# Fourteen instead of thirteen of the sixteen pairs of the second mixer matrix by products over halves, and an earlier fetch of the gate tiles' weights

## The chip, the cores and the metric

The kernel runs on one core of a Trainium2 chip. The metric is the device time of one execution in microseconds (us); less is better. Before the change, three runs gave 1724.98 us in the median (1724.34 to 1728.57).

## The reference

One step of a decoder layer for 1024 prompt tokens and 8 x 4 sample tokens, that is 1056 tokens together, with a model width of 1024. Everything is float32.

```
h  = RMSNorm(x);  p = h @ w_in        # columns: q | k | v | conv input | z | a | b | gate_A | gate_B
branch A: stick-breaking attention, 8 heads x 64, strictly causal
branch B: short conv + SiLU, gated delta rule, 4 heads with a 128x128 state
m = sigmoid(gate_A) * (o_A @ w_pa) + sigmoid(gate_B) * (o_B @ w_pb);   x = x + m @ w_o
x = x + relu(RMSNorm(x) @ w_up)^2 @ w_down                             # 1024 -> 4096 -> 1024
y = RMSNorm(x)
```

gate_A and gate_B are 1024 columns each. The two matrices of the channel mixer, w_up (1024 x 4096) and w_down (4096 x 1024), are what most of the change is about.

## The kernel before, in words

**A dense product.** Each float32 operand is split into a rounded part and the rest (ScalarE copies to the rounded type, VectorE subtracts), and a product is three TensorE matmuls for each block of 128 of the contraction: high x high, high x low, low x high. This is `dense`, L134 to L139, so nearly all matmuls of the program have one of the lines L137, L138, L139, and the tile names tell the stages apart: `pd_g` gate tiles, `sc`/`wt`/`po` attention, `pb`/`pa` the merge, `px` out projection, `pu` w_up, `pw` w_down by products, `pv` w_down directly. Results go to PSUM banks, and ScalarE or VectorE empties these.

**Gate tiles.** The sixteen 128-column tiles of gate_A and gate_B go through `proj_steps` (L232): the first step of a tile calls `load_w` (L118), which takes a staging tile (tag `wst`, one buffer), issues the DMA on SyncE's queue (L123) and then splits into `wh` and `wl` (L127 on ScalarE, L128 on VectorE, two buffers each, so the split of a tile needs the matmuls of the tile two before it to be done). Then come 4 token blocks of 24 matmuls each; each result goes through a sigmoid on ScalarE (L1042), and the tile is stored (L1044). The first eleven tiles stand ahead of the attention's main loop; the other five are "fills", cut into steps and spread over 34 attention blocks (`pipeline`, L1028). `stage_a` computes the scores four blocks ahead of their use; with a head's first block it loads that head's q, k and v (`attn_load` L914 with the DMAs of L923 to L925, `load_v` L964, its DMA L966), and ScalarE empties the scores through a sigmoid (L939). `residual_step` brings x in (L1049) and writes it out transposed. The order of the instructions on each engine comes from the program's order, from priorities (`tc.high_priority()`) and from a list scheduler that runs a timeline model; each engine and SyncE's DMA queue then take their instructions strictly in that order.

**w_up.** The 32 column tiles of 128 hidden units form 16 pairs (f, f+16), and the tokens come in two groups g. For the pairs from 3 on in both groups, and for the first three with g = 1, both halves of the contraction, of the hidden units and of the tokens are combined into 7 products over halves in the place of 8 (Strassen in Winograd's form, `up_products` L1373). The first NPL = 3 pairs are done directly for g = 0 (`up_plain`, L1332), because the pools of the products aren't there yet. What follows is relu and square (L1394, L1395). For the pairs from NPL on, four VectorE subtractions (L1399 to L1402) make the seven combinations of the hidden values that the w_down products need, stored to DRAM as `hc_d` (L1403). The first three pairs are stored as plain hidden values, `h_d`.

**w_down.** The 13 pairs from 3 on are done in groups of 4, 4 and 5 pairs (L1527): for each of the 7 products i, the group's combinations are loaded (`load_h`, L1455 with the DMA of L1457, split at L1452/L1453), the weights are loaded by quarter (L1465), combined (L1472 to L1476) and split (`weight_part` L1470, L1479/L1480), and 8 PSUM tiles accumulate over the pairs of the group; VectorE adds them to `acc` or `ys`. The buffers: 12 tiles for the combinations, 8 for the split weights, 5 for each quarter. In the first group, a load waits its turn behind the earlier one (`queued`), and the loads of product 0 are issued by GpSimd. The other six tiles (pairs 0 to 2) follow directly: weights loaded and split at L1586 to L1588, hidden values `hp`, then four token stages of 8 column blocks with 18 matmuls each (`pv`), each stage followed by the final norm, the transposes (`fin`) and the store.

Of the kernel before, what the change touches and what calls it, by code (L numbers as in the profile page):

```python
# [8 lines left out]
F32 = mybir.dt.float32  # L9
# [9 lines left out]
P = 128  # L19
D = 1024  # L20
# [18 lines left out]
def hybrid_step(ctx, tc, x_prompt, x_sample, cache_k, cache_v, page_table, state_conv, state_ssm,  # L39
# [78 lines left out]
    def load_w(src, name, wp=wpool, st=None):  # L118
        nk = 8 if st is not None else src.shape[1]
        if st is None:  # L120
            st = wp.tile([P, 8, P], F32, tag="wst", name=f"ws_{name}", bufs=1)
            stv = st if nk == 8 else st.rearrange("p a b -> p (a b)").rearrange("p (k c) -> p k c", k=nk)
            wq[0] = SY.dma_start(stv, src)  # L123
        hi = wp.tile([P, 8, P], F32R, tag="wh", name=f"wh_{name}")
        lo = wp.tile([P, 8, P], F32R, tag="wl", name=f"wl_{name}")
        with tc.high_priority():
            S_.activation(hi, st, AF.Copy)  # L127
            V.tensor_tensor(lo, st, hi.bitcast(F32), op=ALU.subtract)  # L128
        if nk != 8:
            hi = hi.rearrange("p a b -> p (a b)").rearrange("p (k c) -> p k c", k=nk)  # L130
            lo = lo.rearrange("p a b -> p (a b)").rearrange("p (k c) -> p k c", k=nk)
        return hi, lo
# [96 lines left out]
                      [xhc[c][:, k] for k in range(KT)], [xlc[c][:, k] for k in range(KT)], n)  # L229
                evac(c, o, n, pt)  # L230

    def proj_steps(col, name, evac, done):  # L232
        ws = []

        def step(c, o, n):
            if not ws:
                ws.append(load_w(winv[:, :, col:col + P], name))
            wh, wl = ws[0]
            pt = dtile(f"pd_{name}_{c}", True)
            dense(pt, [wh[:, k] for k in range(KT)], [wl[:, k] for k in range(KT)],  # L240
                  [xhc[c][:, k] for k in range(KT)], [xlc[c][:, k] for k in range(KT)], n)
# [795 lines left out]
    def gate_steps(j, b):  # L1037
        gt = fk.tile([P, T], F32, tag="ft", name=f"gt{b}_{j}", bufs=NFT)

        def ev(c, o, n, pt):  # L1040
            with tc.high_priority():
                S_.activation(gt[:, o:o + n], pt[:, :n], AF.Sigmoid)  # L1042

        return proj_steps(3592 + b * D + j * P, f"g{b}_{j}", ev, lambda: SY.dma_start((gA_d, gB_d)[b][j], gt))  # L1044

    def residual_step(t):
        n = P if t < 8 else NS
# [172 lines left out]
    wuv = w_up[0].rearrange("(k p) n -> p k n", p=P)  # L1220
    wdv = w_down[0].rearrange("(k p) n -> p k n", p=P)
    h_d = dr.tile([FF // P, P, T], F32, name="h_d")
    NPL = 3
    hc_d = dr.tile([FF // P // 2 - NPL, 7, P, HN], F32, name="hc_d")

    def by_group(ap, g):
        return ap.rearrange("p (h g n) -> p g h n", h=2, g=2)[:, g]
# [100 lines left out]
    def next_bank(name):  # L1328
        bank[0] += 1
        return mk4[bank[0] % 4](name)  # L1330

    def up_plain(f, g):  # L1332
        wh, wl = load_8(wuv[:, :, f * P:(f + 1) * P], f"up{f}")
        t = up_.tile([P, 7, QN], F32, tag="t", name=f"tp{f}{g}")[:, 0:2]
        for h, (i, ii) in enumerate(((0, 1), (7, 6))):
            pt = next_bank(f"pu{f}{g}_{h}")
            dense(pt, wh, wl, [Xh[g][i][:, k] for k in range(4)] + [Xh[g][ii][:, k] for k in range(4)],
                  [Xl[g][i][:, k] for k in range(4)] + [Xl[g][ii][:, k] for k in range(4)], QN)
            S_.activation(t[:, h], pt[:, :QN], AF.Relu)
        S_.activation(t, t, AF.Square)  # L1340
        SY.dma_start(by_group(h_d[f], g), t)

    def up_weights(f):
        a = wop.tile([P, 8, P], F32, tag="wh", name=f"ua{f}")
# [28 lines left out]
    def up_products(w7, f, g):  # L1373
        pts = []
        for i in range(7):
            pt = next_bank(f"pu{f}{g}_{i}")
            dense(pt, w7[i][0], w7[i][1], [Xh[g][i][:, k] for k in range(4)], [Xl[g][i][:, k] for k in range(4)], QN)
            pts.append(pt[:, :QN])
        p1, p2, p6, p7, p5, p4, p3 = pts

        t = up_.tile([P, 7, QN], F32, tag="t", name=f"t{f}{g}")
        u1, u2 = t[:, 2], t[:, 5]
        S_.activation(u1, p1, AF.Copy)
        with tc.high_priority():
# [5 lines left out]
            V.tensor_tensor(t[:, 1], u2, p4, op=ALU.subtract)  # L1390
            V.tensor_tensor(t[:, 3], p3, u1, op=ALU.add)
        rows = (t[:, 0:4:3], t[:, 1:7:5])
        for r in range(2):
            S_.activation(rows[r], rows[r], AF.Relu)  # L1394
            S_.activation(rows[r], rows[r], AF.Square)  # L1395
            if f < NPL:
                SY.dma_start(by_group(h_d[f + NF * r], g), rows[r])
        if f >= NPL:
            V.tensor_tensor(t[:, 4], t[:, 3], t[:, 0], op=ALU.subtract)  # L1399
            V.tensor_tensor(t[:, 3], t[:, 6], t[:, 3], op=ALU.subtract)  # L1400
            V.tensor_tensor(t[:, 2], t[:, 6], t[:, 4], op=ALU.subtract)
            V.tensor_tensor(t[:, 5], t[:, 2], t[:, 1], op=ALU.subtract)  # L1402
            SY.dma_start(hc_d[f - NPL, :, :, g * QN:(g + 1) * QN].rearrange("i p n -> p i n"), t)  # L1403

    out_proj(0)
    blocks(0)
# [10 lines left out]


    norm(1)
    for f in range(NPL):  # L1420
        up_plain(f, 0)
        up_plain(f + NF, 0)
    kxctx.close()
    u7a = pool("u7a", stack=uctx)
    for f in range(NPL, NF):
        w7 = up_weights(f)
        for g in range(2):
            up_products(w7, f, g)
        if f < 2 * NPL:
            up_products(up_weights(f - NPL), f - NPL, 1)  # L1430
    uctx.close()
    xg_ctx[1].close()
    woctx.close()
# [90 lines left out]
            last_q[0] = r if hasattr(r, "ins") else hq[0]  # L1524
        return r

    groups = [list(range(3, 7)), list(range(7, 11)), list(range(11, 16))]  # L1527
    for gi, fs in enumerate(groups):
        qs2 = [quarters(f) for f in fs]
        if gi:  # L1530
            for q, f in zip(qs2, fs):
                for nm in PARTS:
                    queued(lambda: load_part(q, f, nm), False)
        for i in range(7):

# [12 lines left out]
            if gi == 0 and i == 0:  # L1548
                ys[:] = [fp.tile([P, T], F32, name=f"y{j}") for j in range(KT)]
            if gi == 0 and i in YLOAD:  # L1550
                j0, h = YLOAD[i]
                for j in range(j0, j0 + HJ):
                    queued(lambda: SY.dma_start(half(ys[j], h), half(x1_d[j], h)))
            for j in range(HJ):
                if gi == 0 and i in (0, 2, 3, 4):
                    acc[i, j] = acp.tile([P, HN], F32, name=f"acc{i}_{j}")
                cs_ = slice(j * P, (j + 1) * P)
                for n in range(2):
                    ns_ = slice(n * QN, (n + 1) * QN)
                    pt = next_bank(f"pw{gi}{i}_{j}{n}")  # L1560
                    dense(pt, [w[:, 0, cs_] for w in ws], [w[:, 1, cs_] for w in ws], [h[:, 0, ns_] for h in hs],
                          [h[:, 1, ns_] for h in hs], QN)
                    dst = targets(i, j)[:, ns_]
                    with tc.high_priority():
                        if gi == 0 and i in (0, 2, 3, 4):
                            S_.activation(dst, pt[:, :QN], AF.Copy)
                        elif i == 5:
                            V.tensor_tensor(dst, dst, pt[:, :QN], op=ALU.subtract)
                        else:
                            V.tensor_tensor(dst, pt[:, :QN], dst, op=ALU.add)  # L1570
                if gi == len(groups) - 1:
                    combine(i, j)
# [94 lines left out]
```

## Time and profile before

| | us |
|---|---|
| median of three runs | 1724.98 |
| the profiled execution, its own time | 1733.34 |
| its span, first to last instruction | 1731.6 |
| TensorE busy in the span | 1682.5 |
| VectorE busy | 1153.2 |
| ScalarE busy | 773.3 |
| GpSimd busy | 200.4 |

The profiled execution is one run under the profiler. Times in its rows count from the start of its span. "PE" is TensorE's matmuls, "PEld" its weight loads, DVE VectorE, ACT ScalarE, POOL GpSimd, SPq SyncE's DMA queue. A matmul's recorded duration (283 ns at 264 columns) is longer than the distance to the next one, since matmuls are pipelined; the distance is read from a window (time over count). A row of a wait names the waiting engine, its tile and line, what it waited for, the sum, the number of waits and the longest. In rows of a timeline, the bracket at the end is the engine's idle time ahead of that instruction and what ended it.

### The profile page before, as it was taken

How to read it: one execution, taken by the hardware profiler on the slowest of the kernel's cores; microseconds unless marked ns; L12 is line 12 of the kernel's file. 1: busy time of each engine (PE TensorE's matmuls, PEld its weight loads, DVE VectorE, ACT ScalarE, POOL GpSimd, SP SyncE). 2: the span in 40 equal slices, each digit the busy share in tenths (PEclk: the TensorE clock that was granted, in tenths of full speed). 3: DMA queues.
4: the chain of work that ended last, by engine and by line, in shares of the span. 5: the costliest groups of instructions: out<-in, count | busy, mean ns of one | idle time of the engine just before them, and what ended most of it. 6: DMA issues, size and time to landing. Idle time of an engine off the chain costs nothing.

```text
span 1731.6 us, 34630 instructions
## 1 busy us (share of the span) xinstructions
PE 1682.5 (97%) x13958; PEld 1624.7 (94%) x13958; DVE 1153.2 (67%) x2309; ACT 773.3 (45%) x1542; POOL 200.4 (12%) x243
## 2 busy tenths in 40 slices
PE   7999999999998999999999999999999999999998
PEld 6999999999998788988989989999999999999998
DVE  6665677867243317778766487887777679788743
ACT  5553434343324214564443456554454564344353
POOL 1120111110005114444400000000000000000000
PEclk9999999999999999999999999999999999999999
DMA  5142233234346478977134645555443766433411
GB/s 179 44 122 69 67 107 92 93 118 133 119 138 211 131 185 200 209 196 193 32 118 125 179 140 145 149 148 160 152 137 113 259 217 218 148 117 95 136 68 66
DMA packets 259036, 239.24 MB, mean 138 GB/s; under 512 B 55890, under 2 KB 217011, under 8 KB 258876
## 3 DMA queue, kind: packets, MB, share of 16 engines
q1 hardware_dynamic: 253926, 226.27, 43.9%
q0 software_dynamic: 3200, 10.52, 1.9%
q8 instruction: 110, 1.80, 0.4%
q10 hardware_dynamic: 1750, 0.23, 0.1%
q14 instruction: 50, 0.41, 0.1%
HBM read 163.21 MB, written 73.77 MB: 137 GB/s over the span
## 4 chain that ended last, share of the span: by engine, by line
PE 88%; DMA 4%; DVE 4%; issue 2%; ACT 1%; SPq 0%; DVEq 0%; POOLq 0%; ACTq 0%
PE pu L139 6%; PE pu L137 6%; PE pu L138 6%; PE pw L139 5%; PE pw L138 5%; PE pw L137 5%; PE pd_g L137 3%; PE pd_g L139 3%; PE pd_g L138 3%; PE wt L111 2%; PE po L985 2%; PE pv L137 1%; PE pv L139 1%; PE pv L138 1%; PE px L138 1%
## 5 line engine op out<-in xcount | busy, mean ns | idle before, releaser
L139 PE MATMUL pu<-Xh,ul 128*128 128x264 f32 x812 | 230.1, 284 | 0.0
L137 PE MATMUL pu<-Xh,uh 128*128 128x264 f32 x812 | 229.8, 283 | 0.0
L138 PE MATMUL pu<-Xl,uh 128*128 128x264 f32 x812 | 229.7, 283 | 0.0
L137 PE MATMUL pw<-hc,w 128*128 128x264 f32 x728 | 204.1, 284 | 2.4 <-ACT w L1479 2.4
L138 PE MATMUL pw<-hc,w 128*128 128x264 f32 x728 | 204.6, 285 | 0.0
L139 PE MATMUL pw<-hc,w 128*128 128x264 f32 x728 | 200.8, 285 | 1.0 <-DVE w L1480 1.0
L137 PEld LDWEIGHTS pu<-Xh,uh 128*128 128x128 f32 x812 | 153.2, 189 | 0.1
L138 PEld LDWEIGHTS pu<-Xl,uh 128*128 128x128 f32 x812 | 152.6, 188 | 0.0
L137 PE MATMUL pd_g<-xh,wh_g 128*128 128x256 f32 (+1 forms) x512 | 150.6, 294 | 1.5 <-issue 1.5
L139 PEld LDWEIGHTS pu<-Xh,ul 128*128 128x128 f32 x812 | 152.0, 188 | 0.0
L138 PE MATMUL pd_g<-xl,wh_g 128*128 128x256 f32 (+1 forms) x512 | 149.4, 292 | 1.8 <-issue 1.8
L139 PE MATMUL pd_g<-xh,wl_g 128*128 128x256 f32 (+1 forms) x512 | 149.6, 292 | 1.1 <-issue 1.1
L137 PEld LDWEIGHTS pw<-hc,w 128*128 128x128 f32 x728 | 136.8, 188 | 2.6 <-ACT w L1479 2.6
L138 PEld LDWEIGHTS pw<-hc,w 128*128 128x128 f32 x728 | 136.2, 188 | 0.0
L139 PEld LDWEIGHTS pw<-hc,w 128*128 128x128 f32 x728 | 134.3, 188 | 1.4 <-DVE w L1480 1.4
L947 DVE TENSOR_TENSOR_SCAN pr<-am 128x127 f32<-128x127 f32 (+7 forms) x64 | 87.9, 1376 | 42.7 <-POOL am L943 42.6
L139 PEld LDWEIGHTS pd_g<-xh,wl_g 128*128 128x128 f32 x512 | 98.0, 191 | 5.9 <-issue 5.7
L137 PEld LDWEIGHTS pd_g<-xh,wh_g 128*128 128x128 f32 x512 | 97.9, 191 | 4.7 <-issue 4.0
L138 PEld LDWEIGHTS pd_g<-xl,wh_g 128*128 128x128 f32 x512 | 97.9, 191 | 2.6 <-issue 2.0
L1479 ACT ACTIVATE w<-a 128x512 fp32r<-128x512 f32 x78 | 43.4, 620 | 88.4 <-PE pw L139 77.0
L139 PE MATMUL px<-mh,wl_wo 128*128 128x264 f32 x256 | 72.4, 285 | 1.3 <-DVE wl_wo L1231 1.2
L138 PE MATMUL px<-ml,wh_wo 128*128 128x264 f32 x256 | 72.6, 285 | 0.0
(577 smaller groups left out, 5071.1 us busy)
## 6 DMA issues: line engine op xcount, KB each, us to landing
hc_d<-t SPq DMA_DIRECT2D x26, 924.0 KB
hc<-hc_d SPq DMA_DIRECT2D x87, 264.0 KB
a<-in_w_down_dram SPq DMA_DIRECT2D x48, 256.0 KB
ws_g<-in_w_in_dram SPq DMA_DIRECT2D x16, 512.0 KB
ws_wo<-in_w_o_dram SPq DMA_DIRECT2D x32, 256.0 KB
ua<-in_w_up_dram SPq DMA_DIRECT2D x16, 512.0 KB
ub<-in_w_up_dram SPq DMA_DIRECT2D x16, 512.0 KB
gA_d<-gt SPq DMA_DIRECT2D x8, 528.0 KB
```

Source lines behind the costliest of these rows:

```text
L111: PE.transpose(out, in_, ident[:k, :k])
L137: PE.matmul(pt[:, :n], lhsT=wh[k], rhs=xh[k], start=(k == 0), stop=False)
L138: PE.matmul(pt[:, :n], lhsT=wh[k], rhs=xl[k], start=False, stop=False)
L139: PE.matmul(pt[:, :n], lhsT=wl[k], rhs=xh[k], start=False, stop=(k == nk - 1))
L947: V.tensor_tensor_scan(pr[:, n - 1:0:-1], am_r, am_r, 1.0, op0=ALU.mult, op1=ALU.bypass)
L985: PE.matmul(po[64 * r:64 * r + 64, 0:P], lhsT=vn[:, b, rs], rhs=wts[hh, 2 * m + r][:, b * P:(b + 1) * P], start=(b == 0), stop=(b == 2 * m ...
L1479: S_.activation(tl[:, 0], src, AF.Copy)
```

## The change

Two edits in one. First, NPL is split: NPU = 3 says how many pairs of w_up are done directly for g = 0, as before; NPL = 2 says from which pair on w_down goes by products, so pair 2 moves from the direct part to the products (14 pairs in groups of 4, 5 and 5). `up_plain` therefore does both tiles of a pair in one call and, for pair 2, makes the combinations. The weights' splits of the first product of the first group get high priority. Second, the gate tiles' weights: after the split of one tile, the DMA of the next one is issued at once (in the program's order), not at the first step of the next tile.

```diff
-    def proj_steps(col, name, evac, done):
+    ahead_w = {}
+
+    def fetch_w(col):
+        ahead_w[col] = wpool.tile([P, 8, P], F32, tag="wst", name=f"ws_c{col}", bufs=1)
+        SY.dma_start(ahead_w[col], winv[:, :, col:col + P])
+
+    def proj_steps(col, name, evac, done, next_col=None):
         ws = []

         def step(c, o, n):
             if not ws:
-                ws.append(load_w(winv[:, :, col:col + P], name))
+                if col not in ahead_w:
+                    fetch_w(col)
+                ws.append(load_w(None, name, st=ahead_w[col]))
+                if next_col is not None:
+                    fetch_w(next_col)
...
-    NPL = 3
+
+    NPU, NPL = 3, 2
...
+    def combos(f, g, t):
+        V.tensor_tensor(t[:, 4], t[:, 3], t[:, 0], op=ALU.subtract)
+        V.tensor_tensor(t[:, 3], t[:, 6], t[:, 3], op=ALU.subtract)
+        V.tensor_tensor(t[:, 2], t[:, 6], t[:, 4], op=ALU.subtract)
+        V.tensor_tensor(t[:, 5], t[:, 2], t[:, 1], op=ALU.subtract)
+        SY.dma_start(hc_d[f - NPL, :, :, g * QN:(g + 1) * QN].rearrange("i p n -> p i n"), t)
+
     def up_plain(f, g):
...
+        t = up_.tile([P, 7, QN], F32, tag="t", name=f"tp{f}{g}")
+        rows = (t[:, 0:4:3], t[:, 1:7:5])
+        for r in range(2):
+            wh, wl = load_8(wuv[:, :, (f + NF * r) * P:(f + NF * r + 1) * P], f"up{f}{r}")
...
+            S_.activation(rows[r], rows[r], AF.Square)
+            if f < NPL:
+                SY.dma_start(by_group(h_d[f + NF * r], g), rows[r])
+        if f >= NPL:
+            combos(f, g, t)
...
-    for f in range(NPL):
+    for f in range(NPU):
         up_plain(f, 0)
-        up_plain(f + NF, 0)
...
-    groups = [list(range(3, 7)), list(range(7, 11)), list(range(11, 16))]
+    groups = [list(range(2, 6)), list(range(6, 11)), list(range(11, 16))]
...
-            ws = [weight_part(q, f, i) for q, f in zip(qs2, fs)]
+            with tc.high_priority() if gi == i == 0 else ExitStack():
+                ws = [weight_part(q, f, i) for q, f in zip(qs2, fs)]
```

More of the change, by code (lines that the diff above doesn't have):

```diff
@@ L1042, in ev, with col @@
                 S_.activation(gt[:, o:o + n], pt[:, :n], AF.Sigmoid)
-        return proj_steps(3592 + b * D + j * P, f"g{b}_{j}", ev, lambda: SY.dma_start((gA_d, gB_d)[b][j], gt))
+        def col(j, b):
+            return 3592 + b * D + j * P
+        return proj_steps(col(j, b), f"g{b}_{j}", ev, lambda: SY.dma_start((gA_d, gB_d)[b][j], gt),
+                          None if (j, b) == (KT - 1, 1) else col(*((j, 1) if b == 0 else (j + 1, 0))))
     def residual_step(t):
@@ L1330, in next_bank @@
         return mk4[bank[0] % 4](name)
-    def up_plain(f, g):
[L1333 to L1341, printed above, removed]
+    def combos(f, g, t):
[4 more added lines that the diff above has]
+        SY.dma_start(hc_d[f - NPL, :, :, g * QN:(g + 1) * QN].rearrange("i p n -> p i n"), t)
+    def up_plain(f, g):
+        t = up_.tile([P, 7, QN], F32, tag="t", name=f"tp{f}{g}")
+        rows = (t[:, 0:4:3], t[:, 1:7:5])
+        for r in range(2):
+            wh, wl = load_8(wuv[:, :, (f + NF * r) * P:(f + NF * r + 1) * P], f"up{f}{r}")
+            for h, (i, ii) in enumerate(((0, 1), (7, 6))):
+                pt = next_bank(f"pu{f}{g}{r}_{h}")
+                dense(pt, wh, wl, [Xh[g][i][:, k] for k in range(4)] + [Xh[g][ii][:, k] for k in range(4)],
+                      [Xl[g][i][:, k] for k in range(4)] + [Xl[g][ii][:, k] for k in range(4)], QN)
+                S_.activation(rows[r][:, h], pt[:, :QN], AF.Relu)
+            S_.activation(rows[r], rows[r], AF.Square)
[3 more added lines that the diff above has]
+            combos(f, g, t)
     def up_weights(f):
@@ L1398, in up_products @@
         if f >= NPL:
[L1399 to L1403, printed above, removed]
+            combos(f, g, t)
     out_proj(0)
@@ L1419, in hybrid_step @@
     norm(1)
-    for f in range(NPL):
+    for f in range(NPU):
         up_plain(f, 0)
-        up_plain(f + NF, 0)
     kxctx.close()
     u7a = pool("u7a", stack=uctx)
-    for f in range(NPL, NF):
+    for f in range(NPU, NF):
         w7 = up_weights(f)
@@ L1428, in hybrid_step @@
             up_products(w7, f, g)
-        if f < 2 * NPL:
-            up_products(up_weights(f - NPL), f - NPL, 1)
+        if f < 2 * NPU:
+            up_products(up_weights(f - NPU), f - NPU, 1)
     uctx.close()
```

## The prediction

> **What bounds the kernel now.** I read the page's busy table and its chain first, then windows of the product stages, then TensorE's waits.
>
> ```profile
> PE 1682.5 (97%) x13958; PEld 1624.7 (94%) x13958; DVE 1153.2 (67%) x2309; ACT 773.3 (45%) x1542; POOL 200.4 (12%) x243
> PE 88%; DMA 4%; DVE 4%; issue 2%; ACT 1%; SPq 0%; DVEq 0%; POOLq 0%; ACTq 0%
> ...
> 1410.00:1500.00 90.00, 90.00 (x739) 90.00 (x738) 66.32 (x127) 39.42 (x74) 0.00 (x0) 1.00 0.53 179
> 1500.00:1640.00 140.00, 140.00 (x1149) 140.00 (x1148) 119.02 (x228) 57.15 (x96) 0.00 (x0) 1.00 0.37 118
> ...
> PE sc L937 <- ACT s L939: 4.2, 1, 4.2
> PE pw L137 <- ACT w L1479: 2.4, 1, 2.4
> PE pw L139 <- DVE w L1480: 1.0, 2, 0.5
> PE pv L137 <- ACT wd L1587: 0.9, 2, 0.7
> PE pv L139 <- DVE wd L1588: 0.3, 1, 0.3
> ```
>
> TensorE bounds it: 97% busy, 88% of the chain. So an edit pays in two ways only: fewer matmuls, or a TensorE wait that goes. In the two windows of w_down's products TensorE is never idle, and a matmul of 264 columns comes every 90.00/739 = 0.1218 us (140.00/1149 gives the same). Five rows of waits lie where the change touches the program: 4.2 us in the attention's start, 2.4 and 1.0 in the first group of w_down, 0.9 and 0.3 at the start of its direct part.
>
> A wait can cost more than its length:
>
> ```profile
> 652.60:656.00 3.40, 3.03 (x13) 2.84 (x13) 2.17 (x3) 2.13 (x5) 2.76 (x4) 0.50 0.80 122
> ...
> 1652.60:1656.00 3.40, 3.40 (x17) 3.40 (x17) 1.77 (x6) 1.88 (x4) 0.00 (x0) 0.52 0.00 0
> ```
>
> The seventh number is the granted clock. Right after the 4.2 us wait, and right after those of the direct part, stand 3.4 us at half clock: in the second, 17 matmuls instead of some 28. At half clock, the busy 3.03 us of the first cost about 1.5 us, and the 3.40 of the second (clock 0.52) 1.6.
>
> **Part 1: the matmuls of pair 2.**
>
> ```profile
> L137 PE MATMUL pw<-hc,w 128*128 128x264 f32 x728 | 204.1, 284 | 2.4 <-ACT w L1479 2.4
> L137 PE MATMUL pv<-hp,wd 128*128 128x264 f32 x192 | 55.9, 291 | 0.9 <-ACT wd L1587 0.9
> 1359.77 0.43 DVE L1399 TENSOR_TENSOR t<-t 128x264 f32<-128x264 f32 x1 [1.39 <-ACT t L1395]
> hc_d<-t SPq DMA_DIRECT2D x26, 924.0 KB
> 1075.00:1370.00 295.00, 293.13 (x2412) 292.93 (x2412) 220.17 (x480) 146.47 (x258) 4.38 (x8) 1.00 0.49 151
> 1670.54 0.52 ACT L1614 ACTIVATE y<-y,vec 128x264 f32<-128x264 f32 x1
> ```
>
> Three lines of 728 matmuls for 13 pairs are 2184, or 168 a pair; three of 192 for six direct tiles are 576, or 96 a tile. Pair 2 adds 168 and takes away 2 x 96 = 192: 24 fewer, 24 x 0.1218 = **2.9 us**. All of them are on the path.
>
> What comes with it lies beside other work. Eight more subtractions (four for each token group) are 8 x 0.43 = 3.4 us of VectorE in the w_up stage, where it is busy 220 of 295 us; uncovered they'd cost those 3.4. The store of a token group has seven pieces, 924 KB, where the plain hidden values have four of these, 528 KB: 0.8 MB more in all, and the loads grow by the same, under DMA shares of 0.49 and 0.53. At the 151 GB/s of that window it is 5 us each if uncovered. Splits move from the direct part into product stages where ScalarE has half its time free. Groups of 5 are no new load: the window from 1500 to 1640 lies in such a group, and TensorE is full there. New is that two of them follow each other with five buffers for each quarter of the weights, so that none is spare at the change of groups: the last quarter of the second group is split by the start of its seventh product, and the third group needs it for its second product, two products or 2 x 120 x 0.1218 = 29 us later, while five loads of 256 KB at the 179 GB/s of the 1410 window take 7.3; that is the price if the cover fails. In the direct part, a column block shrinks from 18 to 12 matmuls, 1.46 us; ScalarE has two operations for it, of which the longer takes 0.52, so at most 1.04: TensorE still sets the pace. I take nothing for all of these.
>
> **Part 2: the fetch of the gate tiles.** ScalarE and SyncE's queue at the start of the attention:
>
> ```profile
> 616.40 0.37 SPq L123 DMA_DIRECT2D ws_g<-in_w_in_dram  x1
> 626.67 0.38 SPq L966 DMA_DIRECT2D vn<-v_d  x1
> 632.30 0.78 SPq L1049 DMA_DIRECT2D xr<-in_x_prompt_dram  x1
> 633.12 0.47 SPq L923 DMA_DIRECT2D qs<-qh_d  x1
> 637.98 0.45 SPq L925 DMA_DIRECT2D kl<-kl_d  x1
> 639.17 0.39 SPq L123 DMA_DIRECT2D ws_g<-in_w_in_dram  x1
> ...
> 631.08 1.23 DVE L128 TENSOR_TENSOR wl_g<-ws_g,wh_g 128x1024 fp32r<-128x1024 f32 x1 [4.96 <-ACT wh_g L127]
> 642.24 0.73 ACT L939 ACTIVATE s<-sc,sbb 128x128 f32<-128x128 f32 x2
> 651.39 1.06 ACT L127 ACTIVATE wh_g<-ws_g 128x1024 fp32r<-128x1024 f32 x1 [8.42 <-DMA ws_g<-in_w_in_dram]
> ...
> 639.17 12.14 DMA ws_g<-in_w_in_dram
> ...
> 625.00:655.00 30.00, 25.82 (x200) 25.33 (x199) 6.17 (x9) 7.34 (x15) 3.08 (x8) 0.96 0.94 227
> ```
>
> The chain of the 4.2 us: the thirteenth tile's weights are issued at 639.17, behind six loads of the second head (633.12 to 637.98), and land 12.14 us later, since the DMA engines are 0.94 busy at 227 GB/s. ScalarE's split of them is queued ahead of the emptying of the scores (L939) and stands for 8.42 us; TensorE runs out of free banks and waits. The staging buffer had been free since 631.08 + 1.23 = 632.31. With the fetch written right after the split of the tile before, its place is there, ahead of the second head. Six loads of 256 KB, 1.57 MB, at 227 GB/s are 6.9 us: it lands at about 651.3 - 6.9 = 644.4. ScalarE then stands from 642.24 + 0.73 = 642.97 to 644.4, some 1.5 us instead of 8.4, and since 8.4 cost TensorE 4.2, there are 4.2 us of slack: the wait goes, 4.2 + 1.5 = **5.7 us**. The bounds are 0 (the fetch stays where it is) and 5.7.
>
> What it is moved past: the second head's six loads land up to 2.3 us later (0.52 MB at 227 GB/s). Its scores come after the first head's, whose buffers are free for the third head at 668.33, so some 15 us remain:
>
> ```profile
> 668.33 0.45 SPq L924 DMA_DIRECT2D kh<-kh_d  x1
> ...
> 655.00:765.00 110.00, 110.00 (x894) 98.86 (x894) 81.26 (x77) 57.27 (x126) 45.17 (x63) 1.00 0.82 185
> ```
>
> Next late after that is TensorE's own work: from 655 to 765 it is never idle. The last three tiles' loads come sooner too; what they pass on the queue is x and its transposed stores, which only the out projection reads. For the tiles before the thirteenth the edit changes little, since the DMA of the next one already comes right after a split (the one at 616.40, say).
>
> **Part 3: priority for the first splits of w_down.**
>
> ```profile
> 1367.18 0.65 ACT L1394 ACTIVATE t<-t 128x528 f32<-128x528 f32 x1 [3.78 <-DVE t L1390]
> 1369.86 1.13 ACT L1479 ACTIVATE w<-a 128x512 fp32r<-128x512 f32 x2
> 1375.57 5.64 SPq L1465 DMA_DIRECT2D a<-in_w_down_dram  x8
> 1382.23 0.69 DVE L1472 TENSOR_TENSOR s<-a,a 128x512 f32<-128x512 f32 x1 [3.23 <-DMA a<-in_w_down_dram]
> 1405.52 3.10 DVE L1480 TENSOR_TENSOR w<-a,w 128x512 fp32r<-128x512 f32 x5
> 1380.00:1400.00 20.00, 20.00 (x166) 20.00 (x165) 16.24 (x30) 9.37 (x20) 0.00 (x0) 1.00 0.96 349
> ```
>
> Before, ScalarE idles 3.78 us, then empties w_up's last pair, and only at 1369.86 splits the weights that TensorE waits for. With priority the splits fit into that idle time, and the 2.4 us go from there. But the third product, 30 us later, hangs on quarters issued from 1375.57 on; at 1382.23 VectorE waits for these, the DMA engines are 0.96 busy, and VectorE works through to 1405.52, where TensorE waits 1.0 us now. None of this comes sooner, so TensorE, 2.4 us earlier, will wait 2.4 us longer there. I take **0**, between a gain of 3.4 (both waits go) and a loss of 2.3 (four splits of 1.13/2 in front of the emptying of the last pair, which delays its store and the queue behind it).
>
> **Part 4: the start of the direct part.**
>
> ```profile
> 1625.30 14.85 SPq L1586 DMA_DIRECT2D wds<-in_w_down_dram  x9
> 1645.45 0.33 SPq L1586 DMA_DIRECT2D wds<-in_w_down_dram  x1
> ```
>
> Twelve weight loads become eight. They start once w_down's last products let the queue go (1625.30) and went at 14.85/9 = 1.65 us each, so the eighth is issued near 1638.5 instead of 1645.45 for the twelfth, 7 us sooner. The second half's first use comes sooner by 4 blocks of 6 matmuls, 2.9 us. That leaves 4 us against waits of 0.9 + 0.3 = 1.2: they go, and with them the half clock, 1.2 + 1.6 = **2.8 us**; bounds 0 and 2.8.
>
> The Trainium skill, page "TensorE: Matmul & The Clock Gate", section "HAM oscillation — how this bites in real kernels", says that the clock falls to half after an idle gap of more than about 3.4 us. The 4.2 us wait agrees; the 1.2 us in pieces that stand before the window at 1652.6 don't, so the page would look for another cause of that one.
>
> **Sum.** 2.9 + 5.7 + 0 + 2.8 = 11.4 us. The profiled execution took 1733.34 us, its span 1731.6; the median is 1724.98, so 8.4 us of the profiled one aren't in an ordinary run, and a wait or two may be larger in the profile than without it. I subtract from the median and leave that to the range: 1725.0 - 11.4 = **1713.6 us**, and 1710.2 to 1715.9 with the bounds of part 3.
>
> **The rivals.** About 0.3%, 5.2 us, can be told from no change.
>
> - The fetch doesn't get ahead: the scheduler keeps it behind the second head, because in its model the split ends later than it does on the chip. For it: split and first load are 0.8 us apart. Then 2.9 + 2.8 = 5.7: 1719.3. Chance 0.15.
> - The wait of the direct part stays, because hidden values and weights share ScalarE: 2.9 + 5.7, 1716.4. Chance 0.10.
> - The half clock at 1652.6 isn't due to that wait and stays: 1.6 less, 1715.2. Against it: it follows the waits directly. Chance 0.06. This is what the Trainium skill's page, in the section named above, would make of it.
> - Both waits stay: 2.9 alone, 1722.1. Chance 0.11.
> - Slower: the fetch is queued too far ahead. SyncE takes its queue in order; a fetch put ahead of the first head's loads (626.67) stands there until the staging buffer is free at 632.31, and the first head's q, k, v and the x tile behind it come 5.6 us later. TensorE then waits for the first scores, 5.6 + 1.5 for the clock: -2.9 - 2.8 + 7.1, 1726.4. It decides from about 4.2 us of standing. Standing at L123 is seen at both ends:
>
> ```profile
> SPq L123 <- DVE us L346: 68.8, 6, 24.9
> SPq L123 <- DVE wl_g L128: 6.2, 5, 3.2
> ```
>
> Waits for this very split were at most 3.2 us; the longest of any weight fetch was 24.9, which would give 1725.0 - 5.7 + 24.9 + 1.5 = 1745.7. Chance 0.13.
>
> **How the numbers follow.** The forecast keeps 0.45. Faster by over 5.2 us: 0.45 + 0.10 + 0.06, and of the first rival (5.7 us) 0.09: 0.70. Within: the rest of that, 0.06, the 0.11 and about half of the last, 0.06: 0.23. Slower: 0.07. The range, 1709.5 to 1725.5, holds the forecast with its bounds and four rivals, and leaves out most of the fifth.
>
> **What would show it.** 2352 `pw` and 384 `pv` matmuls at 0.122 us; the thirteenth `ws_g` issued near 632 to 633 and no `sc` wait of 4 us; clock 1.0 from 650 to 660; no `pw` wait at the first product, but 2 to 3 us at the third; no `pv` waits for `wd`. I am wrong if a new TensorE wait of over 3 us stands anywhere, or if the thirteenth fetch still follows the second head's loads.

## The result, and the profile after

In runs beside the kernel before, the changed kernel took 1715.79 us (median of 5; the kernel before 1726.84): the ratio of times is 0.9929, 95% interval 0.9916 to 0.9943. By the medians 11.05 us are gone, by the ratio 12.3 (9.8 to 14.5); the forecast was 11.4. A later set of the changed kernel holds one execution of 5709.03 us, which no trace explains and no ratio includes. The profiled execution took 1711.77 us, its span 1710.1. The busy table and the chain of its page:

```profile
PE 1670.7 (98%) x13934; PEld 1615.8 (94%) x13934; DVE 1166.7 (68%) x2327; ACT 775.9 (45%) x1548; POOL 215.4 (13%) x243
...
PE 84%; DVE 6%; DMA 4%; issue 2%; POOL 2%; ACT 1%; SPq 1%; DVEq 0%; POOLq 0%; ACTq 0%
```

TensorE still bounds it, with 13934 matmuls in place of 13958: the 24 that should go. The spans of the two profiled executions lie 21.5 us apart, twice the medians' difference, so stages aren't compared by this pair alone: the kernel before was run again (the last experiment) and its second span is 1721.8.

TensorE's waits in the changed kernel (engine, tile and line, what it waited for: us in total, times, longest):

```profile
PE dkt L111 <- DMA kg<-in_cache_k_dram,idx: 3.8, 2, 3.5
PE pw L137 <- ACT w L1501: 2.4, 1, 2.4
...
PE pb L138 <- DVE obl L1140: 1.2, 1, 1.2
PE pw L139 <- DVE w L1502: 1.1, 2, 0.6
...
PE sc L947 <- DMA kh<-kh_d: 0.8, 1, 0.8
```

The 4.2 us wait of `sc` for ScalarE is gone, and so is every wait of `pv`. The two of `pw`, 2.4 at the first product of `w_down` and 1.1 at the third, stand as they stood before (2.4 and 1.0; L1479 and L1480 are now L1501 and L1502). The first row, a wait for gathered keys, is not of the change: the kernel before has it in its second trace too (3.1 in all), and with six staging buffers it is 3.8 there as well. The last row, a wait for a later head's keys, has grown from 0.3; it is taken up again under part 2.

The same kernel's windows (sum; TensorE, its weight load, VectorE, ScalarE, GpSimd busy; granted clock; DMA share; GB/s), at the start of the attention, in the products, and over the whole direct part:

```profile
630.00:650.00 20.00, 20.00 (x157) 19.40 (x156) 10.06 (x12) 7.29 (x16) 7.31 (x12) 1.00 1.00 240
...
1480.00:1640.00 160.00, 160.00 (x1316) 160.00 (x1315) 132.90 (x252) 66.06 (x111) 0.00 (x0) 1.00 0.37 122
1644.00:1699.00 55.00, 55.00 (x464) 55.00 (x463) 29.34 (x71) 33.44 (x71) 2.59 (x3) 1.00 0.16 65
```

TensorE is never idle and its clock is 1.00 in all three. A matmul still takes 160.00/1316 = 0.1216 us: products with two long groups in a row and more loads lost nothing.

Its queue on SyncE at the start of the attention (start, time taken, line, transfer), VectorE's split of the twelfth tile, and ScalarE's timeline:

```profile
624.82 0.44 SPq L935 DMA_DIRECT2D kl<-kl_d  x1
625.40 0.69 SPq L236 DMA_DIRECT2D ws_c<-in_w_in_dram  x1
626.19 1.63 SPq L1063 DMA_DIRECT2D xr<-in_x_prompt_dram  x1
627.87 0.79 SPq L933 DMA_DIRECT2D qs<-qh_d  x1
```

```profile
624.15 1.23 DVE L128 TENSOR_TENSOR wl_g<-ws_c,wh_g 128x1024 fp32r<-128x1024 f32 x1 [4.96 <-ACT wh_g L127]
```

```profile
635.70 1.06 ACT L127 ACTIVATE wh_g<-ws_c 128x1024 fp32r<-128x1024 f32 x1 [3.58 <-DMA ws_c<-in_w_in_dram]
636.96 0.73 ACT L949 ACTIVATE s<-sc,sbb 128x128 f32<-128x128 f32 x2
```

The thirteenth tile's weights are issued at 625.40, as soon as the split of the twelfth is done with the staging buffer (624.15 + 1.23 = 625.38), now ahead of x and of the second head's loads (from 627.87), and land by 635.70, where ScalarE's split of them starts. That split comes before the emptying of the scores (L949), not between two of these as before. ScalarE still stands 3.58 us, but no TensorE wait for it is left.

### The profile page after: what moved, and what is told of

Its sections match the earlier page's. It is cut to its first block, busy times and chain, and to the rows that moved or that the text cites. A ratio compares the mean times of both kernels' runs of the same rounds, so it can differ in the third digit from the quotient of the medians.

```text
span 1710.1 us, 34614 instructions
## 1 busy us (share of the span) xinstructions
PE 1670.7 (98%) x13934; PEld 1615.8 (94%) x13934; DVE 1166.7 (68%) x2327; ACT 775.9 (45%) x1548; POOL 215.4 (13%) x243
## 4 chain that ended last, share of the span: by engine, by line
PE 84%; DVE 6%; DMA 4%; issue 2%; POOL 2%; ACT 1%; SPq 1%; DVEq 0%; POOLq 0%; ACTq 0%
PE pu L139 6%; PE pu L137 6%; PE pu L138 6%; PE pw L139 5%; PE pw L138 5%; PE pw L137 5%; PE pd_g L139 3%; PE pd_g L137 3%; PE pd_g L138 3%; PE wt L111 1%; PE px L138 1%; PE px L137 1%; PE px L139 1%; PE pd_z L137 1%; PE po L995 1%
## 5 line engine op out<-in xcount | busy, mean ns | idle before, releaser
L137 PE MATMUL pw<-hc,w 128*128 128x264 f32 x784 | 219.5, 284 | 2.4 <-ACT w L1501 2.4
L138 PE MATMUL pw<-hc,w 128*128 128x264 f32 x784 | 219.0, 285 | 0.0
L139 PE MATMUL pw<-hc,w 128*128 128x264 f32 x784 | 214.9, 285 | 1.1 <-DVE w L1502 1.1
L137 PEld LDWEIGHTS pw<-hc,w 128*128 128x128 f32 x784 | 147.2, 188 | 2.6 <-ACT w L1501 2.6
L138 PEld LDWEIGHTS pw<-hc,w 128*128 128x128 f32 x784 | 146.3, 188 | 0.0
L139 PEld LDWEIGHTS pw<-hc,w 128*128 128x128 f32 x784 | 144.5, 188 | 1.5 <-DVE w L1502 1.5
L1501 ACT ACTIVATE w<-a 128x512 fp32r<-128x512 f32 x84 | 46.7, 620 | 97.1 <-PE pw L139 86.9
L1474 ACT ACTIVATE hc<-hc 128x528 fp32r<-128x528 f32 x98 | 61.6, 643 | 29.7 <-DMA hc<-hc_d 28.2
```

The source lines that it names most:

```text
L137: PE.matmul(pt[:, :n], lhsT=wh[k], rhs=xh[k], start=(k == 0), stop=False)
L138: PE.matmul(pt[:, :n], lhsT=wh[k], rhs=xl[k], start=False, stop=False)
L139: PE.matmul(pt[:, :n], lhsT=wl[k], rhs=xh[k], start=False, stop=(k == nk - 1))
L1474: S_.activation(tl[:, 0], tl[:, 1].bitcast(F32), AF.Copy)
L1501: S_.activation(tl[:, 0], src, AF.Copy)
```

## The experiments

The theory: four separate edits, of which the fetch takes away the wait at the start of the attention, pair 2 takes away 24 matmuls, the shorter direct part takes away its waits, and the priority gives nothing. Each rival puts the gain of a part elsewhere or denies it.

**The fetch alone**, in the kernel before:

```
-    def proj_steps(col, name, evac, done):
+    def proj_steps(col, name, evac, done, next_col=None):
...
-                ws.append(load_w(winv[:, :, col:col + P], name))
+                if col not in ahead_w:
+                    fetch_w(col)
+                ws.append(load_w(None, name, st=ahead_w[col]))
+                if next_col is not None:
+                    fetch_w(next_col)
```

> The kernel before with the earlier fetch alone. Theory (terms add up): 5.7 us faster, ratio 0.9967; the thirteenth tile's weights are issued right after the split of the twelfth, ScalarE stands less than 4.2 us for them, TensorE's wait for the scores (4.2 us) is gone and with it the half clock behind it; the 1.2 us of waits for the direct part's weights stay. Rival (given back later): the wait goes, but the merge's first matmul comes no sooner, ratio 1.000. Rival (idle alone): 4.2 us, since the half clock isn't tied to the wait, 0.9976.

Measured: 1718.29 us against 1726.4, ratio 0.9956 (0.9943 to 0.9969), that is 7.6 us less (5.4 to 9.8). The forecast's 0.9967 lies in the interval, 0.9976 for the idle time alone doesn't. The wait of `sc` for ScalarE is gone. Of TensorE's waits at the direct part, which this edit doesn't touch, one is left, 0.2 us for ScalarE's splits (`wd`). It was 0.9 in the first trace of before. That wait is marginal: it changes though nothing near it was edited.

**All but the fetch**, the changed kernel with the gate tiles' fetch put back:

```
-        return proj_steps(col(j, b), f"g{b}_{j}", ev, lambda: SY.dma_start((gA_d, gB_d)[b][j], gt),
-                          None if (j, b) == (KT - 1, 1) else col(*((j, 1) if b == 0 else (j + 1, 0))))
+        return proj_steps(col(j, b), f"g{b}_{j}", ev, lambda: SY.dma_start((gA_d, gB_d)[b][j], gt))
```

> The changed kernel without the earlier fetch: pair 2 by products alone. Theory: 2.9 us for 24 matmuls and 2.8 us for the waits at the direct part's start and the half clock behind them, 5.7 us faster than before, ratio 0.9967; the scores' wait of about 4 us is there as before, and so is the half clock behind it. Rival (matmuls alone, a wait as long stands elsewhere): 2.9 us, 0.9983. Rival (no sum, the fetch is what made room): 0 to 1 us.

Measured: 1721.42 us against 1726.4, ratio 0.9969 (0.9957 to 0.998), 5.4 us less. Its waits of TensorE and two of its windows:

```profile
PE sc L947 <- ACT s L949: 3.7, 1, 3.7
...
PE pw L137 <- ACT w L1500: 2.4, 1, 2.4
```

```profile
645.00:651.60 6.60, 5.03 (x22) 4.84 (x23) 4.28 (x5) 3.87 (x8) 4.19 (x6) 0.50 0.90 196
...
1365.20:1368.50 3.30, 3.30 (x17) 3.30 (x16) 2.85 (x6) 2.32 (x5) 0.00 (x0) 0.50 0.92 308
```

The wait of the attention's start is back, with 6.6 us at clock 0.50 behind it in place of 3.4. No `pv` wait is left. The gains of the two halves, 7.6 + 5.4 = 13.0, make up the whole (12.3 by its ratio, 9.8 to 14.5) within the noise: neither half shows a need of the other. New is the second window: behind the 2.4 us wait of `pw`, which stands in every one of these kernels, the clock falls to half here, and in the first trace of before it didn't.

**The fetch for the thirteenth tile only**: as in the first experiment, but only the twelfth of the sixteen jobs is given a next column, so that one load alone is fetched ahead.

```
+                          None if (j, b) != gjobs[11] else col(*((j, 1) if b == 0 else (j + 1, 0))))
```

> The kernel before, with the earlier fetch for the thirteenth gate tile alone; all other tiles are fetched at their first step. Theory: all of the fetch's gain hangs on that tile, so the same as the run with all tiles within 1 us, ratio 0.9967. Rival (every tile's earlier fetch brings a little): half of it or less, 0.998 to 1.000.

Measured: 1719.08 us, ratio 0.9953 (0.9938 to 0.9968), as much as the fetch for all sixteen. The gain of the edit hangs on one of its loads. That rests on the times: the profiled execution of this kernel has a wait that no other trace shows (2.1 us for VectorE at about 706, with 3.4 us at half clock behind it), so its gate stage is less short than those of the other kernels with the new fetch.

**Six staging buffers in the direct part** of the kernel before, in place of three, so that its loads start sooner with nothing else changed:

```
-            st = wlp.tile([P, HD2], F32, tag="wst", name=f"wds{f}_{c}", bufs=3)
+            st = wlp.tile([P, HD2], F32, tag="wst", name=f"wds{f}_{c}", bufs=6)
```

> The kernel before with six instead of three staging buffers for the weights of the direct part, nothing else. Theory: its weight loads wait for these buffers; with six, they come sooner, the 1.2 us of waits go and the half clock behind them too: 2.8 us faster, ratio 0.9984. Rival (the half clock is not due to the wait): waits gone, the clock still at half near the direct part's start, 1.2 us, 0.9993. Rival (ScalarE's order, hidden values in front of weights, is the cause): waits stay, 1.000.

Measured: 1723.63 us against 1726.4, ratio 0.9985 (0.9975 to 0.9995), 2.6 us less. No wait of `pv` is left and no half clock at that place. Taken from the 5.4 us of all but the fetch, that leaves 2.8 for pair 2 and the priority, where 24 matmuls are 2.9; the two intervals are about 2 us wide on each side, so this is only rough. The six buffers' interval also holds 0.9993, the idle time alone; it is the clock, not the time, that speaks against that rival.

**GpSimd for the first high splits.** What the 2.4 us wait at the first product hides: the changed kernel, with the high halves of four of the first group's splits taken from ScalarE.

```
-        S_.activation(tl[:, 0], src, AF.Copy)
+        if i == 0 and f < 6:
+            G.tensor_copy(tl[:, 0], src)
+        else:
+            S_.activation(tl[:, 0], src, AF.Copy)
```

> The changed kernel, with the four first splits of the first group's first product on GpSimd (idle there) in the place of ScalarE; nothing else. Theory (part 3 of the prediction: loads and VectorE bound the third product): TensorE's wait of 2.4 us at the first product goes, the waits at the third product grow from 1.1 by about as much, the time stays within 1 us of the changed kernel (ratio to before 0.9925 to 0.9935). Rival (the first product is the bound, the third has room): 2.4 us faster than the changed kernel, ratio 0.9915.

Measured: 1715.16 us against 1725.03, ratio 0.9933 (0.9914 to 0.9952): the changed kernel's. From its waits:

```profile
PE pw L139 <- DVE w L1505: 2.3, 1, 2.3
```

The wait for ScalarE went, and a wait of 2.3 for VectorE's low half came 4 us later, in the same product; those of the third product (0.6 and 0.5) went with it, where the expectation had them grow. The time stayed, but the place wasn't the one expected, so one more kernel was needed:

**GpSimd for the high and the low halves** of those splits:

```
-        S_.activation(tl[:, 0], src, AF.Copy)
-        V.tensor_tensor(tl[:, 1], src, tl[:, 0].bitcast(F32), op=ALU.subtract)
+        if i == 0 and f < 6:
+            G.tensor_copy(tl[:, 0], src)
+            G.tensor_tensor(tl[:, 1], src, tl[:, 0].bitcast(F32), op=ALU.subtract)
+        else:
+            S_.activation(tl[:, 0], src, AF.Copy)
+            V.tensor_tensor(tl[:, 1], src, tl[:, 0].bitcast(F32), op=ALU.subtract)
```

> The changed kernel with both halves of the four first splits (high and low) on GpSimd. The run with the high half alone moved TensorE's wait of 2.4 us 4 us on, to the low half on VectorE (2.3 us). Theory now: both waits at the first product go; the third product hangs on quarters whose loads are queued behind the store of w_up's last pair, so its waits grow from 1.1 to about 3 and the time stays within 1 us of the changed kernel, ratio to before 0.992 to 0.9935. Rival (the third product has room): 2.4 us faster than the changed kernel, ratio 0.9915 or less, and its waits stay at about 1 us.

Measured: 1714.34 us against 1727.14, ratio 0.9935 (0.9923 to 0.9947). From its waits, and from its timelines of VectorE and SyncE:

```profile
PE pw L138 <- DVE hc L1475: 2.3, 2, 1.5
...
PE pw L137 <- DVE y L1597: 0.6, 1, 0.6
```

```profile
1369.57 0.69 DVE L1494 TENSOR_TENSOR s<-a,a 128x512 f32<-128x512 f32 x1 [4.27 <-DMA a<-in_w_down_dram]
```

```profile
1360.48 0.37 SPq L1352 DMA_DIRECT2D hc_d<-t  x1
...
1364.28 4.19 SPq L1487 DMA_DIRECT2D a<-in_w_down_dram  x8
```

Both waits of the first product are gone, and those of the third have grown from 1.1 to 2.3 + 0.6 us, as expected. VectorE stands 4.27 us for quarters of the weights that are issued only from 1364.28 on, behind the store of the last pair (1360.48). But this kernel delays that store itself. In the changed kernel:

```profile
1356.99 0.37 SPq L1352 DMA_DIRECT2D hc_d<-t  x1
...
1361.00 5.47 SPq L1487 DMA_DIRECT2D a<-in_w_down_dram  x8
```

Counted from the last matmul of `w_up` (starts at 1353.1 there, at 1353.9 here), the store is issued 2.7 us later here, 6.6 us after it in place of 3.9, and the quarters 2.5 us later. The cause is four VectorE subtractions that run beside GpSimd's (last section). The grown waits are 2.9 us in all, so the delay may account for them; that the third product would have held TensorE up without it is not shown.

**Fifteen pairs**: one pair more by products, in groups of 5, the changed kernel's next step.

```
-    NPU, NPL = 3, 2
+    NPU, NPL = 3, 1
...
-    groups = [list(range(2, 6)), list(range(6, 11)), list(range(11, 16))]
+    groups = [list(range(1, 6)), list(range(6, 11)), list(range(11, 16))]
```

> The changed kernel with one more pair by products (15 of 16, groups 5, 5, 5), so that one pair is left for the direct part. Theory: 24 fewer matmuls are 2.9 us again, but a column block of the direct part is 6 matmuls or 0.73 us against 0.94 of ScalarE, so ScalarE sets the pace there: 0.6 us a stage (its 8.8 against 8.2 with the transposes) to 0.21 a block, 2.4 to 6.7 us in all; 0.5 us faster to 3.8 slower than the changed kernel, most likely 1.5 slower. Rival (TensorE alone counts): 2.9 us faster than the changed kernel, ratio to before 0.9912.

Measured: 1716.87 us, ratio to the kernel before 0.9952 (0.9938 to 0.9967); the changed kernel on the same chip, the next run, has 1715.07 and 0.9927 (0.9907 to 0.9947). So with 24 matmuls fewer it is 1.8 us slower by the medians and 4.3 by the ratios, whose intervals overlap: slower by an amount that these runs give only roughly, and not the 2.9 us faster that the matmuls alone would make it. Its waits of TensorE from the products on, its window of the direct part, and the direct part's matmuls in the changed kernel and in this one (duration min/median/max in ns, first to last start):

```profile
PE pw L137 <- ACT acc L1589: 1.8, 1, 1.8
PE fin L111 <- ACT y L1637: 1.0, 4, 0.3
PE pf L1645 <- DVE sa L1636: 0.7, 1, 0.7
```

```profile
1671.00:1708.00 37.00, 35.45 (x278) 34.14 (x276) 26.06 (x67) 27.87 (x69) 2.59 (x3) 0.95 0.21 86
```

```profile
L139 PE MATMUL pv<-hp,wd x128: 279/284/289, 1644.4 to 1698.4; 128*128 128x264 f32 x128
```

```profile
L139 PE MATMUL pv<-hp,wd x64: 279/284/422, 1671.3 to 1705.6; 128*128 128x264 f32 x64
```

The direct part shrinks from 54.0 to 34.3 us, 19.7, where 192 matmuls fewer would be 23.4. The 3.7 us are in its window: 37.00 - 35.45 = 1.6 idle, and a clock of 0.95, which is 0.05 x 37 = 1.9. The idle time is in the rows of `fin` and `pf`: one wait for ScalarE in each of the four stages, 1.0 in all, and 0.7 for VectorE at the end. So ScalarE holds up the ends of the stages; a pace of ScalarE's for every column block, as the expectation had it, isn't seen.

The products are 24.2 us longer (`pw` from first to last start, 312.1 against 287.9) where 168 matmuls are 20.5, again 3.7. Here stands the wait for `acc`. It is in the first group of the products, which now has five pairs; ScalarE's timeline and the window behind the wait:

```profile
1404.62 0.64 ACT L1474 ACTIVATE hc<-hc 128x528 fp32r<-128x528 f32 x1 [1.26 <-DMA hc<-hc_d]
...
1405.69 2.34 ACT L1589 ACTIVATE acc<-pw 128x264 f32<-128x264 f32 x8
```

```profile
1407.00:1410.40 3.40, 3.40 (x17) 3.40 (x17) 1.82 (x3) 2.61 (x7) 0.00 (x0) 0.51 0.18 70
```

Between 1394 and 1410 ScalarE stands 4.9 us in three pieces for loads of the combinations, then empties eight results in a row, and TensorE waits 1.8 us for them: the chain of the attention's start once more. With 3.4 us at half clock behind this wait and another 3.4 behind the one at the first product, which cost 1.7 each, and without the 1.1 of the third product, that is some 4 us. The half clock at the first product is not of this edit: it comes and goes (below).

**The changed kernel again**, unchanged, on the chip of the fifteen pairs:

> The changed kernel once more, beside the two others on the same chip: ratio 0.993 within its interval of 0.9916 to 0.9943. A rival in which the first measurement was luck: 0.996 or more.

Measured: 1715.07 us against 1725.03, ratio 0.9927 (0.9907 to 0.9947). The first result holds.

**The kernel before again**, for a second trace:

> The kernel before, unchanged, for a second trace of it: which of its waits come in every execution. Theory: the scores' wait of about 4 us and the 2.4 us at w_down's first product are there again; the direct part's 1.2 us depends on when loads land and may be smaller; the half clock follows the scores' wait again, for one or two stretches of 3.4 us. Ratio 1.000. A rival in which the first trace was special: no wait for the scores.

Measured: 1725.13 us, ratio 0.9996 (0.9987 to 1.0006). Its waits of TensorE, and its windows behind the first and around the last of these:

```profile
PE sc L937 <- ACT s L939: 3.4, 1, 3.4
...
PE pw L137 <- ACT w L1479: 2.4, 1, 2.4
...
PE pv L139 <- DVE wd L1588: 0.3, 1, 0.3
```

```profile
645.50:648.80 3.30, 3.15 (x13) 2.97 (x14) 2.06 (x3) 1.99 (x6) 2.76 (x4) 0.51 0.72 109
1640.00:1646.00 6.00, 5.44 (x41) 4.86 (x40) 5.36 (x12) 4.83 (x12) 0.00 (x0) 1.00 0.18 68
```

The wait of the attention's start and its half clock are there again. At the direct part TensorE idles 6.00 - 5.44 = 0.6 us in place of 1.2, and the clock stays at 1.00. Behind the 2.4 us wait of `pw` it is at half here (rows under "The clock" below).

## Why the prediction was right, point by point

**Part 1, 2.9 us: right.** The products' and the direct part's groups in the changed kernel (matmuls in each, busy us, mean ns, idle before):

```profile
L137 PE MATMUL pw<-hc,w 128*128 128x264 f32 x784 | 219.5, 284 | 2.4 <-ACT w L1501 2.4
...
L137 PE MATMUL pv<-hp,wd 128*128 128x264 f32 x128 | 36.9, 288 | 0.0
```

That is 3 x 784 = 2352 and 3 x 128 = 384, at an unchanged pace. Three traces without half clock there give the size: from the first `pw` to the last `pv` matmul the fetch alone takes 345.6 us and the changed kernel 342.4 in both of its traces, 3.2 less, of which 0.2 is a wait. What was set down at nothing stayed below 1 us: `w_up` takes 295.7 us from its first to its last matmul in both traces of before, 296.1 and 296.4 in those of the changed kernel. That the step can't simply be repeated is what the fifteen pairs show: 24 matmuls fewer again, and the time went up by 1.8 to 4.3 us.

**Part 2, 5.7 us: the mechanism right, the size a little small.** The gate stage from the first scores to the last gate matmul, in the second trace of before and in the changed kernel:

```profile
L937 PE MATMUL sc<-kh,qs x96: 218/387/796, 635.1 to 862.8; 128*128 128x512 f32 x48, 128*128 128x128 f32 x16, 128*128 128x256 f32 x16, 128*128 128x384 f32 x16
...
L139 PE MATMUL pd_g<-xh,wl_g x512: 274/282/416, 452.1 to 755.4; 128*128 128x256 f32 x128, 128*128 128x288 f32 x43
```

```profile
L947 PE MATMUL sc<-kh,qs x96: 218/387/500, 634.7 to 859.2; 128*128 128x512 f32 x48, 128*128 128x128 f32 x16, 128*128 128x256 f32 x16, 128*128 128x384 f32 x16
...
L139 PE MATMUL pd_g<-xh,wl_g x512: 274/282/582, 452.4 to 749.5; 128*128 128x256 f32 x128, 128*128 128x288 f32 x43
```

755.4 - 635.1 = 120.3 us became 749.5 - 634.7 = 114.8. The mean of the four traces with the old fetch (both of before, all but the fetch, the six staging buffers) is 121.0, that of the traces with the new fetch for all tiles 114.7: 6.3 us, against 4.2 + 1.5. The half clock behind the wait is 3.4 us long in some traces and 6.8 in others, which the first trace of before alone couldn't show. Behind the gate stage the fetch shifts other waits too, which the working didn't have: in the traces with the new fetch for all tiles, a later head's keys keep TensorE 0.8 to 2.6 us (`sc` for the DMA of `kh`; 0.2 to 0.5 with the old one), and the merge's wait for `obl` falls from 2.8 to between 1.1 and 1.5. From the first scores to the last `px` matmul the means are 389.1 and 382.1 us, so 7.0 in all; the fetch alone measured 7.6.

The place of the fetch came as forecast. Times of two traces can't be compared as they stand, since the first scores start at 641.7 in the first trace of before and at 634.7 in the changed kernel's; counted from there, the fetch was to go out 9.4 us ahead (632.31), and went out 9.3 ahead (625.40). It landed 1.0 us behind the first scores where 2.7 were forecast. The step that was off is ScalarE's order: the working left the split behind the first emptying of the scores and had ScalarE stand 1.5 us there. The changed kernel has the split ahead of it, and ScalarE stood 3.58 us, from 632.12 to 635.70, most of it before there were scores to empty. TensorE lost nothing by that, but the 4.2 us of slack were not put to a test.

**Part 3, 0: the sum right, the step to it half wrong.** "With priority the splits fit into that idle time, and the 2.4 us go from there" did not happen. ScalarE's timeline in the changed kernel:

```profile
1352.40 0.65 ACT L1421 ACTIVATE t<-t 128x528 f32<-128x528 f32 x1 [4.91 <-DVE t L1417]
...
1355.09 1.13 ACT L1501 ACTIVATE w<-a 128x512 fp32r<-128x512 f32 x2
```

The splits still come behind the last pair's emptying, and ScalarE idles 4.91 us in front of it, as it did before (3.78): of the priority, this row shows no effect, and no run leaves it out alone. The other half of the argument, that the wait would come back at the third product if it went from the first, is not shown either: with both halves of those splits on GpSimd it did, and the time was the same, but GpSimd's work delayed the third product's loads by about as much. The term was 0 because the wait was never touched.

**Part 4, 2.8 us: the mechanism right, the size that of a bad execution.** Six buffers, which do nothing but bring the loads forward, took the waits away and 2.6 us (0.9 to 4.3) with them. But in the second trace of before these waits are 0.6 us with no half clock, and 0.2 where only the fetch was changed; 2.8 is what they cost in the execution that the prediction read. From its first to its last matmul (`pv`) the direct part of the kernel before takes 81.1 us in the first trace, 78.7 in the second, and 77.3 with six buffers: an ordinary gain of nearer 1.4, which the interval holds as well.

**The clock.** The rival that the half clock at 1652.6 isn't due to the wait has nothing for it: in the traces with 0.6 us of waits there or less, the half clock isn't there either. But the length of a wait alone doesn't decide: the same 2.4 us wait of `pw` had half clock behind it in four traces (the kernel with all but the fetch, the six buffers, the fifteen pairs, the second of before), and none in the first trace of before, in both of the changed kernel, with the fetch alone and with the thirteenth tile's. The stretches are 3.41 us long, or twice, once three times that, and in every trace their starts lie whole multiples of 3.413 us apart (in the first of before, from 652.62 to 1652.72, 293 of them). So each trace gives a raster of windows. Laid over the 2.4 us wait, first in the second trace of before, then in the changed kernel's:

```profile
1358.98:1362.39 3.41, 1.02 (x9) 0.86 (x8) 1.76 (x5) 2.85 (x5) 0.00 (x0) 1.00 1.03 383
1362.39:1365.81 3.42, 3.42 (x18) 3.42 (x17) 3.42 (x7) 2.88 (x6) 0.00 (x0) 0.50 0.88 300
```

```profile
1351.25:1354.66 3.41, 2.10 (x18) 1.90 (x16) 0.87 (x3) 2.06 (x4) 0.00 (x0) 1.00 1.08 370
1354.66:1358.07 3.41, 2.32 (x19) 2.32 (x20) 2.79 (x7) 2.46 (x5) 0.00 (x0) 1.00 1.02 382
1358.07:1361.49 3.42, 3.42 (x31) 3.42 (x30) 3.42 (x7) 3.42 (x7) 0.00 (x0) 1.00 1.02 301
```

In the first, the whole wait lies in one window (3.41 - 1.02 = 2.39 idle), and the next window is at half clock. In the second, it is divided between two (1.31 and 1.09), and none follows. So it is in all nine traces with this wait: 2.3 to 2.5 us idle in one window in the four that have the half clock, at most 1.8 in the five that haven't. The same wait costs 1.7 us more or not, by where it falls on the raster. How much idle time is enough, the traces don't settle: with other waits, 1.8 us in one window had half clock behind them in the first GpSimd kernel and 1.2 at the start of the direct part, and near 575 us four traces have it behind a window without any. The Trainium skill, page "TensorE: Matmul & The Clock Gate", section "HAM oscillation — how this bites in real kernels", asks for an idle gap of more than about 3.4 us; idle times of 1.2 and 2.4 us had half clock behind them here. Its first part, "The HAM clock gate (the "warmup" mystery)", speaks of a free-running window of 4096 cycles, about 3.4 us, and the raster of these traces agrees with it.

**The other rivals.** The fetch that doesn't get ahead, both waits that stay, and the wait of the direct part that stays are excluded by the changed kernel's own rows. The slower rival, a fetch that stands on SyncE in front of the first head's loads, didn't come: the fetch went out behind `kl`. A fetch placed still sooner wasn't tried, so the 4.2 us of standing from which it was to decide stays an estimate.

**The subtraction.** The sum was taken off the median, not off the profiled execution's 1733.34, which would have given 1721.9. That choice was right: the profiled execution of the second trace of before took 1723.48, so the first held some 10 us that are no part of an ordinary run. The time itself, 1713.6, came out 2.2 us too low, most of it because the median of the kernel before is 1.9 higher over five runs than over the three.

**Where luck came in.** Part 2 was forecast some 1 to 2 us too small and part 4 by about as much too large, and part 3's 0 came without the chain that it was argued from. That the sum lies within 1 us of the measured difference is partly because these errors offset each other.

## What to carry to other kernels

An engine that takes its queue in order passes a late load on to work that has nothing to do with it: here a weight split that stood 8.42 us for a DMA held up the emptying of the scores, and issuing that one load ahead of the next head's six was worth more than 24 matmuls. When a wait at the start of a stage is to be removed, ask what sets the next one, and what the engine that takes the work over slows down: at the first product of `w_down` the wait went from ScalarE to VectorE, then to the third product, whose loads the edit itself had delayed, and the time stayed. A saving of the kind "one more of the same" is to be checked at every stage that it loads as well as at the one that it shortens: the fifteenth pair took 24 matmuls away again, and waits and half clock of some 7 us came in their place, half of it in the first group of the products.

## What the runs showed of the hardware that was not expected

VectorE's subtractions of 264 columns, 0.43 us each in the trace of before, while GpSimd did the low halves of the splits (the last experiment on GpSimd; its VectorE and its GpSimd timeline):

```profile
1357.44 1.52 DVE L1350 TENSOR_TENSOR t<-t 128x264 f32<-128x264 f32 x1
1359.00 1.41 DVE L1351 TENSOR_TENSOR t<-t 128x264 f32<-128x264 f32 x1
```

```profile
1353.36 1.29 POOL L1503 TENSOR_TENSOR w<-a,w 128x512 fp32r<-128x512 f32 x1
...
1357.20 2.93 POOL L1503 TENSOR_TENSOR w<-a,w 128x512 fp32r<-128x512 f32 x2
```

1.52 and 1.41 us are 0.43 and 1.0 to 1.1 more, most of the length of one GpSimd subtraction (1.29): VectorE seems to wait for one of these to end (the two subtractions ahead took 0.74 and 0.73). The Trainium skill, page "SBUF — State Buffer", in its list of terms, says that the two engines share a pair of ports, and that the one who holds it keeps it for the full instruction; these rows agree.

The loads under full DMA are slow: the thirteenth tile's 512 KB took 12.14 us before and 635.70 - 625.40 = 10.3 after, at 227 GB/s (625 to 655) and 273 (625 to 636). Moving it ahead in the queue shortened it little, and brought it sooner by its place above all.
